# A one-core gated encoder block: the activation sums of h for the last stage move from the two-tile pool `t6` to the large pool

## The chip, the cores and the metric

The kernel runs on one core of a Trainium2 chip. The metric is device time in microseconds (us) of one execution. Before the change the median of three runs is 1447.47 us (1447.43 to 1447.57).

The engines have short names here. PE is TensorE (matmul) and PEld its loading of the stationary operand; DVE is VectorE; ACT is ScalarE; POOL is GpSimd; SP is SyncE, which issues most of the transfers. "PSUM" is the memory that matmuls write, "SBUF" the one that all other tiles lie in.

## The reference, cut to what matters

The block has 256 tokens of 2048 channels. Everything ahead of the feed-forward part (a gated recurrence, chunked attention, two projections and a merge) is untouched by the change and is left out:

```python
x = x + jnp.einsum('btd,de->bte', merged, w_out[l])
h = rms_norm(x, norm_ffn[l])
gate_up = jnp.einsum('btd,df->btf', h, w_ffn_in[l])      # 2048 -> 2 x 5632
ff_gate, ff_up = jnp.split(gate_up, 2, axis=-1)
x = x + jnp.einsum('btf,fd->btd', jax.nn.silu(ff_gate) * ff_up, w_ffn_out[l])
```

All arrays are float32.

## The kernel before

**The work.** Nearly all of it is matrix products of 256 tokens with weights that stream in once from device memory. A weight matrix is cut into blocks of 512 columns and chunks of 512 rows (four k-tiles of 128). A chunk of a block arrives in two transfers of 512 KB, issued by SP into `raw` tiles (pool `wraw`, eight tiles, line 124). To keep float32 precision with a fast matmul type, every operand is split into a high and a low part: ACT writes the high part (`whi`, lines 141 and 171) and DVE the low part, the difference (`wlo`, lines 142 and 172). The pools `whi` and `wlo` have four tiles each. A product of a k-tile is then three matmuls: high by high, high by low, low by high (lines 162 to 164, or 216 to 218 in `triple`).

**The feed-forward stage.** `hidden` has 11 blocks of 512 columns, `j` = 0 to 10. For each `j` the gate block and the up block are multiplied with x2 (the normalized input of the stage, tiles `x2Th`, `x2Tl`), and `hn` = silu(gate) * up results. For `j` in `SEVEN_IN` = (1, 3, 5, 7, 9) the two blocks are computed together by `product_pair`; for the others one after the other by `product` (lines 162 to 164). Then `transpose_split` transposes `hn` on PE (line 279) and splits it into `hTh` and `hTl`, which the last stage reads. It is a generator: each call of `tick` inside a product runs it one step further, so its steps lie beside the matmuls of the next `j`.

**Seven products for eight.** In `product_pair` the first two k-tiles of a chunk, the two halves of the tokens and the two column blocks form a 2x2 by 2x2 block product, done with seven products where eight are usual. For that, sums of weights and sums of activations are needed. `weight_forms` makes the sums of weights on DVE (line 188) from two `raw` tiles:

```python
        ta = t6_p.tile([P, 2, 512], F32, tag="t6", name=nm("ta"))
        tb = t6_p.tile([P, 2, 512], F32, tag="t6", name=nm("tb"))
        op(ta[:, 0, :], b12, b11, ALU.subtract)
        op(ta[:, 1, :], b22, b12, ALU.subtract)
        p5, p7 = halves(ta)
        op(tb[:, 0, :], ta[:, 0, :], b22, ALU.subtract)
        op(tb[:, 1, :], b21, tb[:, 0, :], ALU.add)
        p6, p4 = halves(tb)
```

`halves` splits each sum into `whi` (ACT) and `wlo` (DVE). Every pair of `SEVEN_IN` has four chunks, so four `ta` and four `tb`, and these take the two tiles of the pool `t6` in turn.

**The activation sums.** The last stage (`w_fo`) uses seven products for the chunks `j` in `SEVEN` = (1, 2, 3, 5, 6, 7, 9). The sums of h that it needs are made by `act_forms` when `hn` is transposed: one copy on ACT (line 325), four small sums on DVE (line 319) into a tile `sf`, then the split of `sf` into the tile `sform`, high part by ACT (line 171), low part by DVE (line 172). POOL's queue then writes `sform` to a buffer `kept` in device memory (line 309), and the last stage reads it back (line 846). A tile `sform` lives from its split to the landing of that write.

**The pools.** `big` has 33 tiles of 4 KB a partition, all with the tag `t4`; it holds x2, h, the sums `fx` of x2 and most else. `t6` has two tiles; before the change `sform` takes one of these two (line 836), the same that `ta` and `tb` take.

**What sets the order.** The program is written for a scheduler that orders each engine's instructions by priority and by when a tile of their pool is free; each engine then works through its own list in order and waits at semaphores. So the pool of a tile changes both what waits for what and where instructions stand. Of the seven `sform`, those of `j` = 2 and `j` = 6 come right ahead of a pair (`j` = 3 and `j` = 7), so that they are made while that pair's weight sums are made. `j` = 0, 4 and 8 make none, so the pairs 1, 5 and 9 begin without one.

Of the kernel before, what the change touches and what calls it, by code (L numbers as in the profile page):

```python
# [11 lines left out]
F32R = mybir.dt.float32r  # L12
# [5 lines left out]
P = 128  # L18
# [24 lines left out]
def block_kernel(ctx: ExitStack, tc: tile.TileContext, x, x_t, w_in, w_pa, w_pb, w_out, w_fi, w_fo,  # L43
# [8 lines left out]
    t6_p = ctx.enter_context(tc.tile_pool(name="t6", bufs=2))  # L52
# [7 lines left out]
    def nm(s):  # L60
        uid[0] += 1
        return f"{s}_{uid[0]}"

    def t4(shape, s, dt=F32):
        return big.tile(shape, dt, tag="t4", name=nm(s))
# [46 lines left out]
    def start(g):  # L112
        running.append(g)
# [33 lines left out]
    def product(w, nb, n_chunks, act, prologue=None, last=False):  # L147

        ps = [mm.tile([P, 512], F32, tag="mm", name=nm("mm")) for _ in range(2)]
        for kc in range(n_chunks):  # L150
            if prologue is not None:
                ws = load_weights(w, nb, kc, 1 if kc < 2 else 2, prologue(kc))
            else:
                with tc.high_priority(offset=min(PREP_AHEAD, tc.cur_priority - first_block[0])):
                    ws = load_weights(w, nb, kc)
            order = [(k4, m) for k4 in range(4) for m in range(2)]
            if last and kc == n_chunks - 1:
                order = [(k4, m) for m in range(2) for k4 in range(4)]
            for n, (k4, m) in enumerate(order):
                wh, wl = ws[k4]  # L160
                ah, al = act(kc * 4 + k4, m)
                nc.tensor.matmul(ps[m], lhsT=ah, rhs=wh, start=kc == 0 and k4 == 0, stop=False)  # L162
                nc.tensor.matmul(ps[m], lhsT=ah, rhs=wl, start=False, stop=False)  # L163
                nc.tensor.matmul(ps[m], lhsT=al, rhs=wh, start=False,  # L164
                                 stop=kc == n_chunks - 1 and k4 == 3)
                if n % 4 == 3:
                    tick()
        return ps
# [101 lines left out]
    def split_tiles(s):  # L270
        return (t4([P, 4, T], s + "h", F32R), t4([P, 4, T], s + "l", F32R))
# [29 lines left out]
    def transpose_split(nat, hi, lo, gain=None, wait=2, pool=aux, forms=None, spill=None):  # L301
        for _ in range(wait):
            yield 1
        for pair in range(2):
            pt = transpose_split_pair(nat, pair, hi, lo, gain, pool)
            if forms is not None and pair == 0:
                act_forms(pt, forms, gain)
                if spill is not None:
                    nc.gpsimd.dma_start(out=spill, in_=forms.bitcast(F32))
            yield 1  # L310
# [485 lines left out]
    def up_times(hn, m, up):  # L796
        nc.vector.scalar_tensor_tensor(out=hn[:, m, :], in0=up, scalar=r2[:, m:m + 1],
                                       in1=hn[:, m, :], op0=ALU.mult, op1=ALU.mult)

    def swiglu_pair(j):  # L800
        hn = t4([P, 2, 512], "hn")
        u = []

        def sums(ub):
            u.extend(t2([P, 512], "u") for _ in range(2))
            nc.scalar.copy(hn[:, 0, :], ub[1])
            add(u[0], ub[6], hn[:, 0, :])
            add(hn[:, 1, :], ub[7], u[0])
            add(u[1], ub[5], hn[:, 1, :])
            add(u[0], ub[5], u[0])  # L810

        cb = product_pair(w_fi, (j, NJ + j), 4, act_x2, fx, aux, mm, sums, plain_first=True,
                          last=True)
        for m in range(2):
            add(hn[:, m, :], cb[m, 0], hn[:, m, :])
            nc.scalar.activation(hn[:, m, :], hn[:, m, :], AF.Silu, scale=r2[:, m:m + 1])
        for m in range(2):
            add(u[m], cb[m, 1], u[m])
            up_times(hn, m, u[m])
        return hn  # L820

    for j in range(NJ):
        if j in SEVEN_IN:
            hn = swiglu_pair(j)
        else:
            ps = product(w_fi, j, 4, act_x2)
            hn = t4([P, 2, 512], "hn")
            for m in range(2):
                nc.scalar.activation(hn[:, m, :], ps[m], AF.Silu, scale=r2[:, m:m + 1])
            ps = product(w_fi, NJ + j, 4, act_x2)  # L830
            for m in range(2):
                up_times(hn, m, ps[m])
        hT.append(split_tiles("hT"))
        f = spill = None
        if j in SEVEN:
            f = t6_p.tile([P, 2, 4, P], F32R, tag="t6", name=nm("sform"))
            spill = kept[j] = dram.tile([P, 2, 4, P], F32, tag=f"kept{j}", name=nm("kept"))
        soon = dict(wait=0, pool=mm) if j + 1 in SEVEN_IN else {}
        start(transpose_split(hn, *hT[j], forms=f, spill=spill, **soon))
# [101 lines left out]
```

## Time and profile before

| | |
|---|---|
| median of 3 runs | 1447.47 us (1447.43 to 1447.57) |
| the profiled execution, its own time | 1449.29 us |
| span of its instructions | 1447.5 us |
| mean granted TensorE clock (1 is 2.4 GHz) | 0.995 |
| PE busy | 1431.1 us, 99% of the span |
| DVE, ACT, POOL busy | 990.4, 749.2, 48.5 us |
| transfers | 287.32 MB, mean 198 GB/s |

The span runs from the first instruction to the last; the execution's own time is 1.79 us longer, for what lies around it. Busy times of different engines overlap. Matmuls are pipelined: a matmul of 512 columns is recorded with 0.39 us, while the next one starts about 0.23 us after it, so an idle time between two records is about 0.16 us less than the distance of their starts lost.

### The profile page before, as it was taken

To read this page: it belongs to the slowest core of one execution; us is meant where nothing else is said; L and a number is where in the kernel's file an instruction comes from. 1 tells how busy PE (TensorE), PEld (TensorE's weight loads), DVE (VectorE), ACT (ScalarE), POOL (GpSimd) and SP (SyncE) were. 2 spreads that over 40 slices of the span, in tenths; PEclk is the share of its full clock that TensorE was granted. 3 is DMA by queue.
4 is the path that set the end of the run, shared out by engine and by line. 5 is a ranking of instruction groups with operands and counts; after the bars stand their busy time and mean duration, and the time that the engine had idled before them with its cause. 6 is when DMAs were issued, how large, how long until landed. Compare 5 with 4: busy or idle time off the path is not lost.

```text
span 1447.5 us, 17485 instructions
## 1 busy us (share of the span) xinstructions
PE 1431.1 (99%) x6484; PEld 1185.8 (82%) x6484; DVE 990.4 (68%) x1225; ACT 749.2 (52%) x966; POOL 48.5 (3%) x59
## 2 busy tenths in 40 slices
PE   8999999999999999999999999999999999999998
PEld 7888888888888888888888877888778888888887
DVE  6768869564654555556658768687686876777876
ACT  6756655555544444445555535455354554454553
POOL 0100100100000000100000000000000001000000
PEclk9999999999999999999999999999999999999999
DMA  9654454456556665556655646656466578666662
GB/s 356 235 196 154 137 198 148 168 172 207 181 198 203 203 192 191 189 183 218 204 194 177 227 150 213 208 178 228 147 216 207 178 236 314 230 200 224 203 190 85
DMA packets 81526, 287.32 MB, mean 198 GB/s; under 512 B 9120, under 2 KB 9376, under 8 KB 81440
## 3 DMA queue, kind: packets, MB, share of 16 engines
q1 hardware_dynamic: 78272, 274.66, 57.1%
q0 software_dynamic: 3168, 11.54, 2.1%
q8 instruction: 51, 0.84, 0.2%
q14 instruction: 35, 0.29, 0.1%
HBM read 278.30 MB, written 7.86 MB: 198 GB/s over the span
## 4 chain that ended last, share of the span: by engine, by line
PE 88%; issue 9%; DMA 1%; DVE 1%; ACT 0%; SPq 0%; POOL 0%; DVEq 0%; ACTq 0%; POOLq 0%
PE mm L162 19%; PE mm L164 19%; PE mm L163 19%; PE mp L216 9%; PE mp L217 9%; PE mp L218 9%; PE bank L279 2%; PE bank L537 1%; DMA xt<-in_x_t 1%; DMA kept<-sform 0%; PE bank L567 0%; PE bank L613 0%; PE bank L664 0%; ACT whi L171 0%; DVE tb L188 0%
## 5 line engine op out<-in xcount | busy, mean ns | idle before, releaser
L142 DVE TENSOR_TENSOR wlo<-raw,whi 128x1024 fp32r<-128x1024 f32 (+1 forms) x340 | 411.5, 1215 | 283.8 <-ACT whi L141 283.4
L141 ACT CAST whi<-raw 128x1024 fp32r<-128x1024 f32 (+1 forms) x340 | 352.9, 1042 | 384.6 <-PE mm L164 332.1
L162 PE MATMUL mm<-whi,xTh 128*128 128x512 f32 x704 | 276.9, 397 | 2.5 <-ACT whi L141 2.5
L164 PE MATMUL mm<-whi,xTl 128*128 128x512 f32 x704 | 274.9, 390 | 0.0
L163 PE MATMUL mm<-wlo,xTh 128*128 128x512 f32 x704 | 274.8, 390 | 0.0
L172 DVE TENSOR_TENSOR wlo<-raw,whi 128x1024 fp32r<-128x1024 f32 (+1 forms) x168 | 183.2, 1112 | 37.9 <-ACT whi L171 37.2
L171 ACT CAST whi<-raw 128x1024 fp32r<-128x1024 f32 (+1 forms) x168 | 157.0, 965 | 98.8 <-PE mp L218 53.6
L162 PEld LDWEIGHTS mm<-whi,xTh 128*128 128x128 f32 x704 | 132.1, 188 | 29.4 <-ACT whi L141 3.6
L164 PEld LDWEIGHTS mm<-whi,xTl 128*128 128x128 f32 x704 | 132.2, 188 | 27.6
L163 PEld LDWEIGHTS mm<-wlo,xTh 128*128 128x128 f32 x704 | 132.3, 188 | 26.9 <-DVE wlo L142 0.9
L162 PE MATMUL mm<-whi,x2Th 128*128 128x512 f32 x384 | 150.0, 391 | 0.0
L164 PE MATMUL mm<-whi,x2Tl 128*128 128x512 f32 x384 | 149.5, 389 | 0.0
L163 PE MATMUL mm<-wlo,x2Th 128*128 128x512 f32 x384 | 149.4, 389 | 0.0
L217 PE MATMUL mp<-wlo,hTh 128*128 128x512 f32 x282 | 109.7, 389 | 0.0
L218 PE MATMUL mp<-whi,hTl 128*128 128x512 f32 x282 | 109.6, 389 | 0.0
L216 PE MATMUL mp<-whi,hTh 128*128 128x512 f32 x282 | 99.7, 390 | 0.0
L218 PE MATMUL mp<-whi,x2Tl 128*128 128x512 f32 x220 | 87.5, 398 | 0.0
L217 PE MATMUL mp<-wlo,x2Th 128*128 128x512 f32 x220 | 87.4, 397 | 0.0
L164 PEld LDWEIGHTS mm<-whi,x2Tl 128*128 128x128 f32 x384 | 72.1, 188 | 15.0
L163 PEld LDWEIGHTS mm<-wlo,x2Th 128*128 128x128 f32 x384 | 72.1, 188 | 14.8
L162 PEld LDWEIGHTS mm<-whi,x2Th 128*128 128x128 f32 x384 | 72.1, 188 | 14.8
L216 PE MATMUL mp<-whi,x2Th 128*128 128x512 f32 x220 | 79.7, 405 | 0.0
(221 smaller groups left out, 1898.5 us busy)
## 6 DMA issues: line engine op xcount, KB each, us to landing
raw<-in_w_fi SPq DMA_DIRECT2D x176, 512.0 KB, 4.6
raw<-in_w_in SPq DMA_DIRECT2D x172, 512.0 KB, 4.4
raw<-in_w_fo SPq DMA_DIRECT2D x88, 512.0 KB, 5.0
raw<-in_w_out SPq DMA_DIRECT2D x32, 512.0 KB, 3.6
raw<-in_w_pa SPq DMA_DIRECT2D x16, 512.0 KB, 4.5
raw<-in_w_pb SPq DMA_DIRECT2D x16, 512.0 KB, 4.6
x<-x POOLq DMA_DIRECT2D x8, 512.0 KB, 4.6
kept<-sform POOLq DMA_DIRECT2D x7, 512.0 KB, 4.6
```

Source lines behind the costliest of these rows:

```text
L141: nc.scalar.copy(hi[:, sl, :], src[:, sl, :])
L142: nc.vector.tensor_tensor(out=lo[:, sl, :], in0=src[:, sl, :], in1=hi[:, sl, :].bitcast(F32), op=ALU.subtract)
L162: nc.tensor.matmul(ps[m], lhsT=ah, rhs=wh, start=kc == 0 and k4 == 0, stop=False)
L163: nc.tensor.matmul(ps[m], lhsT=ah, rhs=wl, start=False, stop=False)
L164: nc.tensor.matmul(ps[m], lhsT=al, rhs=wh, start=False, stop=kc == n_chunks - 1 and k4 == 3)
L171: nc.scalar.copy(hi, src)
L172: nc.vector.tensor_tensor(out=lo, in0=src, in1=hi.bitcast(F32), op=ALU.subtract)
L216: nc.tensor.matmul(ps, lhsT=ah, rhs=wh, start=first, stop=False)
L217: nc.tensor.matmul(ps, lhsT=ah, rhs=wl, start=False, stop=False)
L218: nc.tensor.matmul(ps, lhsT=al, rhs=wh, start=False, stop=final)
L279: nc.tensor.transpose(out=pt[:, j, m * P:(m + 1) * P], in_=nat[:, m, c:c + P], identity=ident)
L537: nc.tensor.matmul(pl[:, j, :], lhsT=ek[:, g // 2, (g % 2) * P:(g % 2 + 1) * P], rhs=eq[:, g, :], start=True, stop=True)
```

## The change

The tile `sform` is taken from the large pool, with the same shape and type. Nothing is computed otherwise, and no instruction is added or removed.

```diff
         hT.append(split_tiles("hT"))
         f = spill = None
         if j in SEVEN:
-            f = t6_p.tile([P, 2, 4, P], F32R, tag="t6", name=nm("sform"))
+            f = t4([P, 2, 4, P], "sform", F32R)
             spill = kept[j] = dram.tile([P, 2, 4, P], F32, tag=f"kept{j}", name=nm("kept"))
```

The order of instructions changes at the beginning of the pairs `j` = 3 and `j` = 7, in the same way, and nowhere else; SP's and POOL's lists stay as they are.

On DVE, at the beginning of the pair `j` = 3. `hTl_6764` is the low part of h of `j` = 2, `sf_6827` and `sform_6765` its activation sums; `ta_6890`, `tb_6891` are the weight sums of the pair's second chunk, made from `raw_6882` and `raw_6886`, and `wlo_6903`, `wlo_6909` their low parts. Before:

```order
L289 TENSOR_TENSOR hTl_6764<-bank_6850,hTh_6763 128x512
L319 TENSOR_TENSOR sf_6827<-bank_6820,sf_6827 128x128
L172 TENSOR_TENSOR wlo_6893<-raw_6882,whi_6892 128x1024
L319 TENSOR_TENSOR sf_6827<-bank_6820,sf_6827 128x128
L172 TENSOR_TENSOR wlo_6897<-raw_6886,whi_6896 128x512
L319 TENSOR_TENSOR sf_6827<-bank_6820,sf_6827 128x128 x2
L188 TENSOR_TENSOR ta_6890<-raw_6886,raw_6882 128x512
L188 TENSOR_TENSOR ta_6890<-raw_6886 128x512
L172 TENSOR_TENSOR sform_6765<-sf_6827,sform_6765 128x512
L172 TENSOR_TENSOR wlo_6903<-ta_6890,whi_6902 128x1024
L188 TENSOR_TENSOR tb_6891<-ta_6890,raw_6886 128x512
L188 TENSOR_TENSOR tb_6891<-raw_6882,tb_6891 128x512
```

With the change, on DVE at the same place, from the same h tile's second half on:

```order
L289 TENSOR_TENSOR hTl_6764<-bank_6850,hTh_6763 128x512
L319 TENSOR_TENSOR sf_6827<-bank_6820,sf_6827 128x128
L188 TENSOR_TENSOR tb_6891<-ta_6890,raw_6886 128x512
L172 TENSOR_TENSOR wlo_6893<-raw_6882,whi_6892 128x1024
L319 TENSOR_TENSOR sf_6827<-bank_6820,sf_6827 128x128
L172 TENSOR_TENSOR wlo_6897<-raw_6886,whi_6896 128x512
L319 TENSOR_TENSOR sf_6827<-bank_6820,sf_6827 128x128
L188 TENSOR_TENSOR tb_6891<-raw_6882,tb_6891 128x512
L172 TENSOR_TENSOR wlo_6903<-ta_6890,whi_6902 128x1024
L319 TENSOR_TENSOR sf_6827<-bank_6820,sf_6827 128x128
L172 TENSOR_TENSOR wlo_6909<-tb_6891,whi_6908 128x1024
```

The two `ta_6890` now stand ahead of the first row shown, before the first half of `hTl_6764`; both halves of `tb_6891` stand ahead of `wlo_6903` instead of behind it and behind `sform`; the low part of `sform_6765` comes four rows after the last row shown. On ACT the high part of `sform_6765` moves from ahead of `whi_6902` (from `ta`) to behind `whi_6908` (from `tb`) and the one cast that follows it.

On PE, at the same place (`mp` are the pair's PSUM banks, `fx` the sums of x2; `whi_6802` is from the first chunk's `tb`, `whi_6902` from `ta_6890`, `whi_6908` from `tb_6891`):

```order
 L218 MATMUL mp_6806<-whi_6892,x2Tl_5365 128x512
+L216 MATMUL mp_6867<-whi_6902,fx_5366 128x512
+L216 MATMUL mp_6871<-whi_6902,fx_5366 128x512
 L217 MATMUL mp_6836<-wlo_6897,fx_5366 128x512
 L218 MATMUL mp_6836<-whi_6896,fx_5366 128x512
-L216 MATMUL mp_6875<-whi_6802,fx_5183 128x512
-L217 MATMUL mp_6875<-wlo_6803,fx_5183 128x512
-L218 MATMUL mp_6875<-whi_6802,fx_5183 128x512
-L216 MATMUL mp_6867<-whi_6902,fx_5366 128x512
-L216 MATMUL mp_6871<-whi_6902,fx_5366 128x512
+L216 MATMUL mp_6810<-whi_6908,x2Th_5364 128x512
```

The first matmul that reads `whi_6908` now takes the place in PE's list that the last of the three matmuls with `whi_6802` and `wlo_6803` had: as many matmuls lie ahead of it as lay ahead of that one.

## Rows read from the trace of the kernel before

**Rows 1.** The page, busy time of each engine, share of the span, instructions.

```profile
PE 1431.1 (99%) x6484; PEld 1185.8 (82%) x6484; DVE 990.4 (68%) x1225; ACT 749.2 (52%) x966; POOL 48.5 (3%) x59
```

**Rows 2.** Waits of the whole span: engine, tile, releaser: total us, times, longest us.

```profile
PE mp L216 <- ACT whi L171: 7.8, 4, 3.0
...
DVE tb L188 <- DMA kept<-sform: 3.1, 2, 1.6
```

**Rows 3.** Windows, pairs j=1,3,5,7: length, busy PE PEld DVE ACT POOL, clock, DMA share, GB/s.

```profile
764.95:819.06 54.11, 54.11 (x243) 44.55 (x242) 46.15 (x55) 30.66 (x34) 0.00 (x0) 1.00 0.61 198
851.25:913.35 62.10, 57.75 (x243) 46.33 (x242) 48.06 (x60) 31.21 (x36) 0.53 (x1) 0.95 0.55 181
945.52:999.62 54.10, 54.10 (x243) 44.55 (x242) 46.16 (x55) 30.62 (x34) 0.00 (x0) 1.00 0.60 200
1031.79:1094.10 62.31, 57.85 (x244) 46.45 (x243) 48.07 (x60) 31.23 (x36) 0.53 (x1) 0.95 0.53 180
```

**Rows 4.** Timeline of PE, pair j = 3: start us, duration us, [idle before, releaser].

```profile
864.20 0.39 PE L218 MATMUL mp<-whi,fx 128*128 128x512 f32 x1
865.54 0.73 PE L216 MATMUL mp<-whi,fx 128*128 128x512 f32 x2 [0.96 <-ACT whi L171]
866.80 0.50 PE L217 MATMUL mp<-wlo,fx 128*128 128x512 f32 x1 [0.53 <-DVE wlo L172]
...
867.61 0.40 PE L218 MATMUL mp<-whi,fx 128*128 128x512 f32 x1
870.87 0.79 PE L216 MATMUL mp<-whi,fx 128*128 128x512 f32 x1 [2.86 <-ACT whi L171]
```

**Rows 5.** Timeline of DVE and ACT, pair j = 3, at the same place.

```profile
860.42 0.28 DVE L319 TENSOR_TENSOR sf<-bank,sf 128x128 f32<-128x128 f32 x1
860.62 1.21 DVE L172 TENSOR_TENSOR wlo<-raw,whi 128x1024 fp32r<-128x1024 f32 x1
...
864.28 0.68 DVE L172 TENSOR_TENSOR sform<-sf,sform 128x512 fp32r<-128x512 f32 x1
...
865.52 1.23 DVE L172 TENSOR_TENSOR wlo<-ta,whi 128x1024 fp32r<-128x1024 f32 x1 [0.56 <-ACT whi L171]
...
868.24 0.69 DVE L188 TENSOR_TENSOR tb<-ta,raw 128x512 f32<-128x512 f32 x1 [1.49 <-DMA kept<-sform]
868.97 0.69 DVE L188 TENSOR_TENSOR tb<-raw,tb 128x512 f32<-128x512 f32 x1
...
869.77 1.04 ACT L171 CAST whi<-tb 128x1024 fp32r<-128x1024 f32 x1 [4.28 <-DVE tb L188]
```

**Rows 6.** Windows in pair j = 3, columns as in rows 3.

```profile
872.00:876.00 4.00, 4.00 (x11) 3.19 (x11) 4.00 (x6) 2.28 (x3) 0.00 (x0) 0.50 0.76 269
877.00:878.00 1.00, 1.00 (x6) 0.80 (x5) 0.28 (x1) 0.00 (x0) 0.00 (x0) 1.00 0.85 283
```

**Rows 7.** Timeline of DVE and ACT, pair j = 5, the corresponding instructions.

```profile
950.78 0.69 DVE L188 TENSOR_TENSOR ta<-raw,raw 128x512 f32<-128x512 f32 x1
...
954.70 0.68 DVE L188 TENSOR_TENSOR tb<-ta,raw 128x512 f32<-128x512 f32 x1
...
957.03 0.68 DVE L188 TENSOR_TENSOR tb<-raw,tb 128x512 f32<-128x512 f32 x1
957.83 1.05 ACT L171 CAST whi<-tb 128x1024 fp32r<-128x1024 f32 x1 [1.23 <-DVE tb L188]
```

**Rows 8.** POOL's last write and first reads of the sums, and their first use on PE.

```profile
1186.17 0.53 POOL L309 DMA_DIRECT2D kept<-sform  x1 [85.73 <-DVE sform L172]
1186.86 2.37 POOL L846 DMA_DIRECT2D sf<-kept  x4 [0.16 <-issue]
...
1225.73 0.39 PE L216 MATMUL mp<-whi,sf 128*128 128x512 f32 x1
```

**Rows 9.** The page, DMA issues: count, KB each, median us to landing.

```profile
kept<-sform POOLq DMA_DIRECT2D x7, 512.0 KB, 4.6
sf<-kept POOLq DMA_DIRECT2D x7, 512.0 KB, 10.7
```

**Rows 10.** An early wait of PE, and the clock around it (timeline; window).

```profile
7.57 0.73 PE L162 MATMUL mm<-whi,xTh 128*128 128x512 f32 x2 [1.76 <-ACT whi L141]
...
6.00:8.00 2.00, 0.43 (x2) 0.30 (x2) 0.96 (x4) 1.07 (x2) 0.00 (x0) 1.00 0.99 306
```

## The prediction, made before the changed kernel was run

> **What bounds the kernel now.** I read first the busy times: PE works 1431.1 of 1447.5 us [rows 1], so only what PE loses by waiting, or by a slower clock, can be won back without taking work away. Next I read the waits of the whole span and look for those whose waiting engine is PE or whose releaser is the tile that the change moves. There are two such lines [rows 2]: PE waits 7.8 us, in four waits, for a high part of weights that ACT writes in `product_pair`; and DVE's sums `tb` wait, twice, 1.6 us at most, for the write of `sform` to device memory.
>
> Third, the windows of the pairs show whether these belong together and what they cost. A pair is the same work each time, so the pairs whose predecessor makes no `sform` are controls for those with one. The controls `j` = 1 and 5 last 54.11 and 54.10 us with a granted clock of 1.00; `j` = 3 and 7 last 62.10 and 62.31 us at 0.95 [rows 3]. The excess over 54.10 is 8.00 and 8.21 us, **16.21 us** in all.
>
> Fourth, the timelines of the pair `j` = 3 take the 8.00 apart. A matmul of the control takes 54.10 / 243 = 0.22 us. PE starts at 864.20, 865.54, 866.80 (two matmuls after the one before), 867.61 and 870.87 [rows 4]: 1.34 - 0.22 = 1.12, then 1.26 - 0.44 = 0.82, then 3.26 - 0.22 = 3.04 us lost, 4.98 together. The missing 8.00 - 4.98 = 3.02 us are the clock: after the long wait PE works at a granted clock of 0.50, that is 1.2 GHz, and by 877 it is back at 1.00, 2.4 GHz [rows 6].
>
> Why PE waits stands on DVE and ACT [rows 5]. DVE makes the low part of `sform` at 864.28, POOL writes it out, and only when that has landed may `tb` of the second chunk take its tile, at 868.24. Its second half follows at 868.97, ACT's cast `whi<-tb` at 869.77, and PE's matmul at 870.87. In the control the second half of `tb` runs at 957.03 and the cast at 957.83 [rows 7]. Moved by 851.25 - 945.52 = -94.27 us, the distance of the two pairs' starts, these are 862.76 and 863.56: six microseconds earlier. The first two losses have the same root: `ta` stands late in DVE's list, because its tile was expected late; in the control it starts at 950.78 [rows 7], 856.51 in the time of `j` = 3.
>
> **The change, part by part.** Instructions and transfers stay the same in number and kind; `sform` takes a tile of `big`, and `ta`, `tb` have `t6` to themselves. All costs are sums against the profiled execution, span 1447.5 us, 1449.29 us with what lies around it; since the excess is a difference inside one span, I take it off the median, 1447.47 us.
>
> *What goes:* the wait of `tb` for the landing, the late `ta`, and the slow clock behind them: 16.21 us, if the pairs 3 and 7 came out as the controls.
>
> *What stays:* they can't come out quite so, since four sums `sf` and the split of `sform` still lie on DVE here, and not in the controls. In the new order three of the sums stand ahead of the second half of `tb`. One takes 0.20 us from start to start (860.42 to 860.62 [rows 5]), so `tb` is 0.60 later than in the control: 863.36, the cast 863.56 + 0.60 = 864.16, its end 1.05 later, 865.21. PE started 0.06 after such a cast (870.87 against 869.77 + 1.04 [rows 4, 5]), so 865.27. In PE's new order the matmul that reads this tile has the place of the one that started at 864.20 [rows 4]. PE loses 1.07 us there, or in parts at one of the waits just ahead. Two sites: **2.14 us**.
>
> Bounds of this term: it is zero if the DVE work is hidden, as in the control; at the most it is the first two losses of before, 1.12 + 0.82 = 1.94 us per site, the nearest rows for a wait on these sums without the transfer. I take 1.07, from the order.
>
> *The rest of the sums.* The fourth `sf` and the low part of `sform` (0.68 [rows 5]) make DVE 0.80 + 0.68 = 1.48 us later than in the control. PE itself is then 1.07 late, so 0.41 is left, and DVE is busy 46.16 of the control's 54.10 us [rows 3], so this is hidden. If that cover is gone it costs 0.41 per site. ACT's cast of `sform` moves behind `whi<-tb`; ACT is busy 30.62 of 54.10 us.
>
> *The spill* is issued some 5 us later, behind the later split. Nobody waits for it now but the last stage, hundreds of microseconds on: nothing.
>
> *POOL's reloads.* The tiles of `big` are handed out in another turn. The fourth of the seven reloads waits, in the new program, for the landing of the last spill: 1186.17 + 4.6 = 1190.8 us, where it was issued by about 1189 [rows 8, 9]. With 10.7 us to land [rows 9] it is there at 1201.5, and PE's first use of any reloaded sum is at 1225.73 [rows 8]. So 24 us cover it: nothing.
>
> *Room in `big`.* At `j` = 9, the fullest, 8 tiles of x2, 20 of h, `hn` and `sform` are alive, 30 of 33; the four `fx` are used up. At `j` = 7 it is 8 + 4 + 16 + 2 = 30. No new wait for room.
>
> **Sum:** 16.21 - 2.14 = 14.07 us less: 1447.47 - 14.07 = **1433.4 us**, with own ends 1447.47 - 16.21 = 1431.3 and 1431.3 + 2 x (1.94 + 0.41) = 1436.0.
>
> **The rivals.**
>
> *The clock falls all the same.* PE would still have a wait at this place of each pair, and if that were enough to drop to 1.2 GHz, each site would keep its 3.02 us: 1436.4 us with one site, 1439.4 with both. For it: the fall of before came behind waits at just this place. Against it: the fall shows behind a loss of 3.04 us that followed 1.94, while at 7.57 us PE had waited 1.76 us and the window around it shows a clock of 1.00 [rows 10]; the wait to come, 1.07, is shorter. Chance 0.09.
>
> The Trainium skill, "TensorE: Matmul & The Clock Gate", section "A second HAM failure mode: psum-queue depth-cycling", speaks against this change's full gain: there, short idles of TensorE between groups of matmuls, while it cycled through PSUM banks, were enough to throw the clock back and forth. By that rule the time would be the 1439.4 of this rival; rows 10 disagree for a single wait of 1.76 us.
>
> *The change doesn't do what it says:* what held `tb` was not the spill but something that ends as late, so that the same wait stands under another name, and the time stays at 1447.5. For it: a wait for several semaphores is put down to the last one alone. Against it: the control makes the same `tb` six microseconds earlier with the same weights' transfers. Chance 0.02.
>
> *Slower: the reload in the last stage.* The spill's tile now belongs to the pool that the reloads draw on, and behind the fourth reload three more and those of x2 stand in POOL's queue. If the last spill landed so late that PE had to wait for a reloaded sum, the time could exceed the old one. Its place is PE's matmul at 1225.73, and it decides when the wait exceeds the 14.07 us saved: the fourth reload would have to land after 1225.73 + 14.07 = 1239.8, 38 us later than worked out above. Slower by that much and 3 more would be 1450.5 us. Spills take 4.6 us, reloads 10.7 [rows 9]; nothing speaks for it. Chance 0.02.
>
> **How the numbers follow.** The forecast has 0.87. A measurement of this kernel tells a change from none at about 0.2%, 2.9 us, that is below 1444.6 or above 1450.4. The forecast and the clock rival lie below, 0.96; the second rival within, 0.02; the third above, 0.02. The range runs from the forecast's lower end to its upper end and takes in the clock's fall at one site: 1431.2 to 1436.5.
>
> **What would show it.** In the profile after, the line of DVE's `tb` waiting for `kept<-sform` is gone; the windows of pairs 3 and 7, found again by their matmuls, last 55.2 us (54.1 to 56.4), with a clock of 1.00; PE's wait for `whi` there is about 1 us once per pair, where three waits stood. The last stage keeps its length. I am wrong if a pair still lasts over 57 us, if the clock falls inside one, if PE waits for a reloaded `sf`, or if another pair than 3 and 7 changes its length.

## The result, and the profile after

| | before | after |
|---|---|---|
| median, same session | 1447.52 us (1447.43 to 1447.62, 4 runs) | 1435.46 us (1435.22 to 1436.35, 4 runs) |
| the profiled execution, its own time | 1449.29 us | 1435.26 us |
| its span | 1447.5 us | 1433.5 us |

The ratio is 0.9918, 95% interval 0.9901 to 0.9935: **12.06 us faster**. Forecast were 14.07 us and 1433.4; the result lies 2.1 us above that, inside the range of 1431.2 to 1436.5. In one later session one execution of the changed kernel took 2219.24 us at a mean granted clock of 0.606; it is left out of what is said there.

The page after, busy time of each engine, answers to [rows 1], and the chain that ended last now runs through PE for 98% of the span, 88% before:

```profile
PE 1425.6 (99%) x6484; PEld 1183.0 (83%) x6484; DVE 989.9 (69%) x1225; ACT 749.1 (52%) x966; POOL 48.5 (3%) x59
...
PE 98%; DVE 1%; ACT 0%; DMA 0%; issue 0%; SPq 0%; DVEq 0%; ACTq 0%
```

The same instructions in number. PE's busy time fell by 1431.1 - 1425.6 = 5.5 us. A matmul is busy for longer at a clock of 0.50, 0.63 us at 872.41 in the trace of before where 0.39 is usual, and in the pairs 3 and 7 those have gone.

The waits of the kernel after: for PE all that the view lists, and of POOL's the one that is new (total us, times, longest us), against [rows 2]:

```profile
PE mm L162 <- ACT whi L141: 1.6, 1, 1.6
PE warm_ps L92 <- DVE warm L89: 1.2, 1, 1.2
PE mp L216 <- ACT whi L171: 1.1, 2, 0.5
...
POOL sf L846 <- DMA kept<-sform: 2.7, 1, 2.7
```

PE's 7.8 us in four waits have become 1.1 in two, none over about half a microsecond, and no `tb` waits for `kept` any more. The last line is the fourth reload of the last stage, which waits for the landing of the last spill, as foretold.

The windows of the five pairs (columns as in [rows 3]; the fifth is `j` = 9):

```profile
764.93:819.02 54.09, 54.09 (x243) 44.55 (x242) 46.16 (x55) 30.62 (x34) 0.00 (x0) 1.00 0.58 197
851.21:906.42 55.21, 54.67 (x243) 44.40 (x242) 47.45 (x60) 31.28 (x36) 0.53 (x1) 1.00 0.61 202
938.59:992.68 54.09, 54.09 (x244) 44.55 (x243) 46.16 (x55) 30.61 (x34) 0.00 (x0) 1.00 0.59 196
1024.85:1080.04 55.19, 54.67 (x243) 44.40 (x242) 47.45 (x60) 31.27 (x36) 0.53 (x1) 1.00 0.63 204
1112.21:1166.33 54.12, 54.12 (x243) 44.55 (x242) 46.16 (x55) 30.62 (x34) 0.00 (x0) 1.00 0.59 197
```

Pairs 3 and 7 went from 62.10 and 62.31 us to 55.21 and 55.19, with a clock of 1.00 throughout; against 54.10 an excess of 1.11 and 1.09 us is left. The other pairs keep their length.

At the kernel's beginning, though, the clock does fall in this profile, where PE has waited 1.64 us (timeline; window):

```profile
7.19 0.73 PE L162 MATMUL mm<-whi,xTh 128*128 128x512 f32 x2 [1.64 <-ACT whi L141]
...
9.00:12.00 3.00, 3.00 (x9) 2.33 (x8) 1.93 (x4) 2.21 (x5) 0.00 (x0) 0.50 1.03 397
```

The kernel before waited 1.76 us there [rows 10] and its clock stayed at 1.00. It costs nothing in the end: the 43rd matmul behind the wait starts at 18.75 us, before at 18.77.

DVE, ACT and PE in pair 3, the kernel after, in order of time; they answer to [rows 4, 5]:

```profile
860.38 0.28 DVE L319 TENSOR_TENSOR sf<-bank,sf 128x128 f32<-128x128 f32 x1
860.58 0.68 DVE L188 TENSOR_TENSOR tb<-ta,raw 128x512 f32<-128x512 f32 x1
...
862.31 0.28 DVE L319 TENSOR_TENSOR sf<-bank,sf 128x128 f32<-128x128 f32 x1
...
863.11 0.28 DVE L319 TENSOR_TENSOR sf<-bank,sf 128x128 f32<-128x128 f32 x1
...
863.31 0.68 DVE L188 TENSOR_TENSOR tb<-raw,tb 128x512 f32<-128x512 f32 x1
...
864.10 1.05 ACT L171 CAST whi<-tb 128x1024 fp32r<-128x1024 f32 x1 [0.68 <-DVE tb L188]
864.27 0.39 PE L218 MATMUL mp<-whi,fx 128*128 128x512 f32 x1
...
865.20 0.50 PE L216 MATMUL mp<-whi,x2Th 128*128 128x512 f32 x1 [0.54 <-ACT whi L171]
...
868.72 0.68 DVE L172 TENSOR_TENSOR sform<-sf,sform 128x512 fp32r<-128x512 f32 x1
```

The first half of `tb` starts at 860.58 instead of 868.24, with nothing to wait for. Three `sf` sums of 0.20 us each stand ahead of the second half, and that makes the cast late and PE with it: 865.20 - 864.27 = 0.93 us from start to start where a matmul takes 0.22, so 0.71 us are lost at this place; the rest of the 1.1 is smaller losses just beside it. The low part of `sform`, and with it the spill, now comes at 868.72, and nobody is waiting for it.

### The profile page after: what moved, and what is told of

The parts are those of the page before. It is cut to its first block, busy times and chain, and to the rows that moved or that the text cites. A ratio compares the mean times of both kernels' runs of the same rounds, so it can differ in the third digit from the quotient of the medians.

```text
span 1433.5 us, 17475 instructions
## 1 busy us (share of the span) xinstructions
PE 1425.6 (99%) x6484; PEld 1183.0 (83%) x6484; DVE 989.9 (69%) x1225; ACT 749.1 (52%) x966; POOL 48.5 (3%) x59
## 4 chain that ended last, share of the span: by engine, by line
PE 98%; DVE 1%; ACT 0%; DMA 0%; issue 0%; SPq 0%; DVEq 0%; ACTq 0%
PE mm L164 21%; PE mm L162 21%; PE mm L163 21%; PE mp L217 10%; PE mp L216 10%; PE mp L218 10%; PE bank L279 2%; PE bank L537 1%; DVE wlo L172 0%; PE bank L567 0%; DMA raw<-in_w_in 0%; ACT whi L171 0%; PE bank L613 0%; PE bank L664 0%; PE bank L692 0%; DVE tb L188 0%
```

## The experiments

Nine kernels ran. The diffs of e1, e2, e4, e5 and e8 are against the kernel before; e6 and e10 are built on the change, and e9 on e6. Two lengths of a pair are used: the window of [rows 3], 54.10 us in a control, and the one from the pair's first matmul to the first matmul of the next plain product, 39.57 us in a control.

My theory was that of the prediction: the landing of the spill holds `tb`; the shared pool also puts `ta` late in DVE's order; both keep PE waiting and the longest of these waits brings the clock down; after the change only the `sf` sums are left. The rivals were that the clock or the landing plays no part of its own, and that it matters which pool the tile comes from.

### e1: the kernel before, once more

No edit: how much does the excess of a pair vary from one execution to the next?

> The kernel before, profiled once more, to see whether its profiled execution (1449.29 us) stands for its ordinary ones (1447.5). Theory: what varies between executions is the slow clock at the pairs 3 and 7. In an ordinary execution the stretches at a clock of 0.50 are shorter, the mean clock is above the 0.995 of the first profile, and the two pairs together exceed 2 x 54.10 us by some 14.4 us (16.21 less the 1.8 that the first profile was longer). Rival: the excess of the pairs is 16.2 us in every execution, and the 1.8 us lie elsewhere, at the kernel's start or end.

Measured: 1447.53 us (1445.88 to 1448.85, 10 runs). Its profiled execution took 1447.62 us. Its pairs 3 and 7, windows:

```profile
851.14:912.16 61.02, 56.62 (x243) 45.38 (x242) 48.08 (x60) 31.22 (x36) 0.53 (x1) 0.97 0.56 183
...
1030.61:1092.39 61.78, 57.31 (x244) 46.03 (x242) 48.07 (x60) 31.22 (x36) 0.53 (x1) 0.94 0.55 181
```

PE's waits are those of [rows 2] to a tenth (7.8, 4, 3.0), but the excess is 6.92 + 7.68 = 14.60 us where the first profile had 16.21. What differs is how long PE worked at the lower clock. Two stretches of pair 3 in this run:

```profile
872.00:874.00 2.00, 2.00 (x5) 1.62 (x6) 2.00 (x3) 1.57 (x2) 0.00 (x0) 0.50 0.73 256
874.00:876.00 2.00, 2.00 (x9) 1.63 (x8) 2.00 (x3) 0.62 (x1) 0.00 (x0) 0.85 0.76 250
```

In the first profile the clock was 0.50 until 876 [rows 6]; here its mean is 0.85 from 874 to 876, so that for most of this stretch it is back at 1.00. So at pair 3 the waits are a fixed cost, 4.98 us in both, and the clock behind them is one that varies: 6.92 - 4.98 = 1.94 us here, 3.02 in the first profile.

### e2: the change for `j` = 2 alone

```diff
-            f = t6_p.tile([P, 2, 4, P], F32R, tag="t6", name=nm("sform"))
+            f = (t4([P, 2, 4, P], "sform", F32R) if j == 2 else
+                 t6_p.tile([P, 2, 4, P], F32R, tag="t6", name=nm("sform")))
```

> Only j = 2 takes its sums from the large pool, j = 6 and the others stay in the two-tile pool. Theory: the sites are independent, so pair 3 lasts about 55.1 us and pair 7 stays at 61 to 62.3, and half of the 12.06 us measured for the whole change goes: 1441.5 us (1440.5 to 1442.5). Rival: the change works through something shared (room in the pool, the order of the last stage): all or nothing, 1435.5 or 1447.5 us.

Measured: 1441.53 us (1440.86 to 1442.77), ratio to before 0.9954 [0.9939, 0.9968], and the windows of pairs 3 and 7:

```profile
850.43:905.61 55.18, 54.66 (x243) 44.40 (x242) 47.47 (x60) 31.27 (x36) 0.53 (x1) 1.00 0.62 202
...
1024.02:1085.86 61.84, 57.38 (x243) 46.07 (x242) 48.07 (x60) 31.25 (x36) 0.53 (x1) 0.94 0.53 181
```

Pair 3 is that of the change, pair 7 that of before: the two sites are independent, and each is worth about half of the gain. Pairs 1, 5 and 9 last 54.07 to 54.09 us, as ever.

### e8: the pool of before, the spill from another tile

```diff
                 if spill is not None:
-                    nc.gpsimd.dma_start(out=spill, in_=forms.bitcast(F32))
+                    nc.gpsimd.dma_start(out=spill.rearrange("p a b c -> p (a b c)"),
+                                        in_=x2T[0][0].rearrange("p a t -> p (a t)").bitcast(F32))
```

> The sums stay in the two-tile pool, but the write to device memory reads a tile of x2 instead (so the last stage multiplies with wrong sums); the sums' tile is free as soon as it is made. Theory: the long wait (3.04 us per site, for the landing) goes, and with it the clock's fall; the late weight sums stay: 1.12 + 0.82 us and up to 1 us more per site, so that the pairs 3 and 7 last 56 to 57.2 us at a clock of 1.00 and the whole 1438 to 1441 us. Rival one, the place in DVE's order is all of it, the landing hides behind it: the pairs stay above 60 us and the time above 1444. Rival two, the landing is all of it: pairs at 55.1 us and 1435.5 us as with the change.

Measured: 1440.87 us (1440.03 to 1441.86), ratio 0.9948 [0.9933, 0.9963]. Pair 3's window, and the start of `ta` on DVE in it:

```profile
853.02:910.57 57.55, 55.21 (x243) 44.32 (x242) 47.89 (x60) 31.18 (x36) 0.00 (x0) 1.00 0.55 186
...
864.85 0.68 DVE L188 TENSOR_TENSOR ta<-raw,raw 128x512 f32<-128x512 f32 x1
```

The same row in the kernel before:

```profile
863.08 0.68 DVE L188 TENSOR_TENSOR ta<-raw,raw 128x512 f32<-128x512 f32 x1
```

PE's matmuls in e8's pair 3 with the three longest of its waits, from the timeline:

```profile
867.32 0.73 PE L216 MATMUL mp<-whi,fx 128*128 128x512 f32 x2 [0.96 <-ACT whi L171]
...
868.66 0.50 PE L217 MATMUL mp<-wlo,fx 128*128 128x512 f32 x1 [0.60 <-DVE wlo L172]
...
870.41 0.50 PE L216 MATMUL mp<-whi,fx 128*128 128x512 f32 x1 [0.56 <-ACT whi L171]
```

Here `ta` stands as late as before: 864.85 - 853.02 = 11.83 us behind the pair's start, before 863.08 - 851.25 = 11.83. The first two waits are 0.96 and 0.60 us, in [rows 4] 0.96 and 0.53; the third is down from 2.86 to 0.56, and the clock stays at 1.00. The excess is 57.55 - 54.10 = 3.45 us in pair 3 and 3.46 in pair 7, a little over what I expected. This splits a site of e1 (7.30 us on average): the landing and the clock that falls behind its wait take 7.30 - 3.45 = 3.85; the late place of `ta` and `tb` on DVE 3.45 - 1.10 = 2.35; and 1.10 are what the change leaves. The split is not quite clean. The first half of `tb` now stands ahead of `wlo<-ta` on DVE, behind it before, and as nothing holds the writes any more they all go out at 669 to 672 us, so that no transfer of sums lies in the pair; the change and e5 have that transfer in the pair and come out at 55.2 us all the same, so its mere presence is not what costs. The pool of a tile costs through the order, too, not through the wait alone.

### e4: each spill issued twice

```diff
                     nc.gpsimd.dma_start(out=spill, in_=forms.bitcast(F32))
+                    nc.gpsimd.dma_start(out=spill, in_=forms.bitcast(F32))
```

> The kernel before with each write of sums to device memory issued twice, so that the tile in the two-tile pool is held until the second has landed. Theory: the landing is on PE's path at the pairs 3 and 7; the second write waits for the first and takes as long (2.9 us from issue to landing), so each of the two pairs grows by 2.5 to 4 us, more where the clock stays low for longer, and the whole by 5 to 9 us: 1453 to 1457 us. Rival: the landing is hidden behind the late weight sums, which alone hold PE: the time stays within 1 us of the kernel before.

Measured: 1453.47 us (1453.08 to 1456.5), ratio 1.004 [1.0027, 1.0053]. The second write goes out when the first has landed, so the tile is held about twice as long. DVE and PE in pair 3, from the timeline:

```profile
871.41 0.69 DVE L188 TENSOR_TENSOR tb<-ta,raw 128x512 f32<-128x512 f32 x1 [5.04 <-DMA kept<-sform]
...
874.04 0.80 PE L216 MATMUL mp<-whi,fx 128*128 128x512 f32 x1 [6.42 <-ACT whi L171]
```

And the pair's window:

```profile
850.87:915.35 64.48, 56.57 (x244) 45.52 (x242) 48.07 (x60) 31.22 (x36) 1.07 (x2) 0.95 0.54 183
```

DVE waits 5.04 - 1.49 = 3.55 us longer than in [rows 5], PE 6.42 - 2.86 = 3.56 longer than in [rows 4], and the pair is 64.48 - 61.02 = 3.46 longer than in e1 (pair 7: 65.07 - 61.78 = 3.29). Microsecond for microsecond the landing is on PE's path. By the medians the two sites together give 5.55 us (1453.47 against 1447.92), less than 2 x 3.55 = 7.1; the varying clock lies in both medians, and whether it is the whole of the difference is not shown.

### e5: a tile of its own, not one of the large pool

```diff
-    big = ctx.enter_context(tc.tile_pool(name="big", bufs=33))
+    big = ctx.enter_context(tc.tile_pool(name="big", bufs=32))
...
+    sform_p = ctx.enter_context(tc.tile_pool(name="sform", bufs=1)); ...
...
-            f = t6_p.tile([P, 2, 4, P], F32R, tag="t6", name=nm("sform"))
+            f = sform_p.tile([P, 2, 4, P], F32R, tag="sform", name=nm("sform"))
```

> The sums of h take neither pool: a pool of their own with one tile, and the large pool gives up one of its 33. Theory: all that counts is that the sums' tile is not one of the two that the weight sums need; the pairs 3 and 7 last 40.65 us as with the change, at a clock of 1.00, and the ratio to before is 0.990 to 0.993. Rival: the change's gain depends on the large pool's many tiles, since the sums of two j follow each other at a distance; then pairs with sums wait for the one tile, or another stage waits for the large pool's 32, and the time is 1437 us or more.

Measured: 1435.27 us (1434.83 to 1435.64), ratio 0.9913 [0.9897, 0.993]; the windows of pairs 3 and 7:

```profile
851.15:906.35 55.20, 54.66 (x243) 44.40 (x242) 47.47 (x60) 31.26 (x36) 0.53 (x1) 1.00 0.62 203
...
1024.79:1080.02 55.23, 54.68 (x244) 44.40 (x242) 47.48 (x60) 31.27 (x36) 0.53 (x1) 1.00 0.62 203
```

This is the change's result. The large pool brings nothing of its own; what counts is that `sform` no longer shares `t6`. The reload's wait for the last spill, which only the large pool can bring, also makes no difference.

### e6 and e9: the sums on POOL

What is left, 1.1 us a site, I put down to the `sf` sums ahead of `tb`. e6 takes them off DVE: ACT copies the transposes out of PSUM, POOL makes the four sums and the low part of `sform`, for all seven `j`.

```diff
-                nc.vector.tensor_tensor(out=out, in0=x, in1=y, op=o)
+                nc.gpsimd.tensor_tensor(out=out, in0=x, in1=y, op=o)
...
+            c = t4([P, 2, T], "pc")
+            nc.scalar.copy(c, pt)
...
+            nc.scalar.copy(f[:, 0], s)
+            nc.gpsimd.tensor_tensor(out=f[:, 1], in0=s, in1=f[:, 0].bitcast(F32),
+                                    op=ALU.subtract)
```

> The change, and in addition the activation sums of h are made by POOL from a copy in a tile of the large pool that ACT writes, so that four small sums and the low part of their split leave DVE, for all seven j. Theory: the wait that is left in the pairs 3 and 7 comes from the three sums ahead of the weight sum on DVE; without them the pairs last 54.1 to 54.4 us, 1.6 to 1.9 us in all less than with the change: 1433.6 us (1433.2 to 1434.5). Rival: POOL's work slows DVE's instructions while both run, or the bank of the transposes comes free later: 1435.5 us or more.

Measured: 1436.3 us (1435.53 to 1436.93), ratio 0.9916 [0.9901, 0.9931]; pair 3 lasts 55.69 us, an excess of 1.59 where the change has 1.11. The expectation failed, though DVE now has five instructions less in the pair (x55). DVE and POOL, in order of time:

```profile
863.62 0.68 DVE L188 TENSOR_TENSOR tb<-raw,tb 128x512 f32<-128x512 f32 x1
863.88 1.58 POOL L338 TENSOR_TENSOR sform<-sf,sform 128x512 fp32r<-128x512 f32 x1 [0.73 <-ACT sform L337]
864.22 2.32 DVE L172 TENSOR_TENSOR wlo<-ta,whi 128x1024 fp32r<-128x1024 f32 x1
866.46 1.21 DVE L172 TENSOR_TENSOR wlo<-tb,whi 128x1024 fp32r<-128x1024 f32 x1
```

DVE's subtraction takes 2.32 us where the next one, of the same shape, takes 1.21. It starts while POOL's subtraction runs, and POOL ends at 863.88 + 1.58 = 865.46, that is 866.54 - 865.46 = 1.08 us ahead of DVE's end: as though it had begun only then. The Trainium skill, "SBUF — State Buffer", section "🔬 SBUF: two separate sides", states that these two engines share a port pair which the one that starts first holds for its whole instruction, and that a DVE operation with two SBUF inputs is blocked by a GpSimd operation that reads SBUF; this pair of rows agrees with it.

e9 tells whether that one instruction of POOL is to blame: it is e6 with the low part of `sform` back on DVE.

```diff
-            nc.scalar.copy(f[:, 0], s)
-            nc.gpsimd.tensor_tensor(out=f[:, 1], in0=s, in1=f[:, 0].bitcast(F32),
-                                    op=ALU.subtract)
+            split(f[:, 0], f[:, 1], s)
```

> As the kernel with all sums on POOL, but the low part of the split stays on DVE, so that POOL has only the four small sums. Theory: in that kernel one DVE subtraction took 2.32 us where others take 1.22, while POOL's subtraction of 128x512 ran (863.88 to 865.46): both engines have two inputs in SBUF and one waits for the other. Without POOL's long instruction the pairs 3 and 7 come out at 40.1 to 40.4 us, against 41.17 with it, and the whole 1.5 to 2 us less than that kernel, 0.6 to 1.2 us less than the change. Rival: the long subtraction was held by something else, and the pairs stay at 41 us or more.

Measured: 1435.1 us (1434.21 to 1435.57), ratio 0.9909 [0.9894, 0.9924]; the pair lasts 55.18 us, or 40.67 to the next plain product, where 40.1 to 40.4 were expected. DVE at the same place:

```profile
860.68 0.78 DVE L188 TENSOR_TENSOR tb<-ta,raw 128x512 f32<-128x512 f32 x1
861.38 2.35 DVE L172 TENSOR_TENSOR wlo<-raw,whi 128x1024 fp32r<-128x1024 f32 x2
863.65 0.68 DVE L188 TENSOR_TENSOR tb<-raw,tb 128x512 f32<-128x512 f32 x1
864.25 1.21 DVE L172 TENSOR_TENSOR wlo<-ta,whi 128x1024 fp32r<-128x1024 f32 x1
865.39 0.68 DVE L172 TENSOR_TENSOR sform<-sf,sform 128x512 fp32r<-128x512 f32 x1
865.99 1.21 DVE L172 TENSOR_TENSOR wlo<-tb,whi 128x1024 fp32r<-128x1024 f32 x1
```

The 2.32 us are 1.21 again, so POOL's long subtraction was the cause in e6. Still the pair gains nothing over the change: the second half of `tb` starts no earlier than with the sums on DVE (863.65 - 851.50 = 12.15 us into the pair, with the change 863.31 - 851.21 = 12.10), and the low part of `sform` now stands ahead of `wlo<-tb`. In the control the two halves of `tb` start 957.03 - 954.70 = 2.33 us apart [rows 7]; here it is 863.65 - 860.68 = 2.97, though no sum lies between them, because two `wlo` of 128x1024 stand there, 2.35 us against the 1.82 of the control's two. Work taken off an engine was replaced by other work at the same place in its list.

### e10 and e11: the sums later, beside the change itself

e10 leaves the sums on DVE and changes when: for `j` = 2 and 6 ACT copies the transposes to a tile of `big`, and the sums are made 14 ticks later. e11 is the change once more, beside it.

```diff
             if forms is not None and pair == 0:
...
+                if wait == 0:
+                    late = t4([P, 2, T], "late")
+                    nc.scalar.copy(late, pt)
...
+        if forms is not None and wait == 0:
+            for _ in range(14):
+                yield 1
+            act_forms(late, forms, gain)
+            nc.gpsimd.dma_start(out=spill, in_=forms.bitcast(F32))
```

> The change, and for j = 2 and 6 ACT copies the transposes to a tile of the large pool and the sums are made from it on DVE in the third and fourth chunk of the pair. Theory: what is left in the pairs 3 and 7 (1.1 us each) is DVE's work on the sums ahead of the second chunk's weight sums; moved behind them the pairs last as those without sums, 39.6 us, and the whole 2.0 to 2.3 us less than the change in this group. Rival: the chunk in which the sums are now made waits instead, pairs at 40.3 us or more and less than 1 us gained.

> The change once more, beside the other kernels of this group and more executions of the kernel before. Theory: the pairs 3 and 7 last 40.7 us from the first matmul of the pair to the next plain product, 1.1 us above the pairs without sums, with no slow clock in them, in every execution; what the ordinary executions of before and after differ by is then the excess of before less 2.2 us, where that excess varies from execution to execution between some 13 and 16 us: a ratio of 0.990 to 0.993.

Measured: e11 1434.56 to 1436.62 us, ratio 0.9908 [0.989, 0.9926], both pairs 55.16 us. e10 1432.77 us (1431.93 to 1433.5), ratio 0.9893 [0.9878, 0.9908]. e10's waits of PE over the whole span:

```profile
PE mm L162 <- ACT whi L141: 1.7, 2, 1.2
PE warm_ps L92 <- DVE warm L89: 1.2, 1, 1.2
```

Its pairs 3 and 5 up to the next plain product, windows:

```profile
850.14:889.70 39.56, 39.56 (x179) 32.59 (x178) 34.34 (x40) 23.34 (x27) 0.00 (x0) 1.00 0.52 179
936.38:975.95 39.57, 39.57 (x179) 32.59 (x178) 34.34 (x40) 22.95 (x26) 0.00 (x0) 1.00 0.53 180
```

Pair 3 is as long as its control, with the same 40 instructions on DVE, and no wait of `product_pair` is left: the sums now run behind the pair, where DVE starts them at 893.66:

```profile
893.66 0.28 DVE L328 TENSOR_TENSOR sf<-late,sf 128x128 f32<-128x128 f32 x1
```

(A window as in [rows 3] holds 247 matmuls of PE in e10's order instead of 243, so the shorter length is compared.) So making and splitting the sums at this place was the whole of the 1.1 us that the change leaves at each site. That it costs through DVE is read from the order of the rows and not shown by e10 alone, which moves ACT's cast of `sform` and the spill along. The mean of e11's four executions is 1435.34 us, 2.6 above e10, of which the pairs give 2 x 1.1 = 2.2; the rest is less than the spread of either. e10 is faster than both kernels.

## Why the prediction was right, point by point

- **What holds `tb`: right.** The line of `tb` waiting for `kept<-sform` is gone, e4 lengthens it and the pair with it, and e8 takes it away alone. The rival that something else ends as late has fallen.
- **"What stays", 1.07 us a site: right**, 1.11 and 1.09 measured. The second half of `tb`, the cast and PE's matmul were put at 863.36, 864.16 and 865.27; they came at 863.31, 864.10 and 865.20, in a pair that begins 0.04 earlier. That it is the work on the sums is shown by e10; that it is DVE's part of it, by the rows alone.
- **"Nothing" for the spill, the reloads and room in `big`: right.** The fourth reload waits 2.67 us for the last spill's landing, and PE's first use of a reloaded sum moved from 1225.73 [rows 8] to 1211.71, by 14.02 us, as the whole did. e5 shows the same without the large pool.
- **The clock rival: fell, but not by the argument against it.** It needed a fall behind waits of about 1 us a pair; the clock was 1.00 there in the change, and also in e8 with 3.45 us lost in several waits of 0.96 at most. Inside the pairs it fell only where one wait was 2.86 us or more. The Trainium skill, "TensorE: Matmul & The Clock Gate", section "A second HAM failure mode: psum-queue depth-cycling", by which short idles between groups of matmuls were enough in another kernel, is not borne out in these pairs. The prediction's argument was that a wait of 1.76 us had left the clock at 1.00 [rows 10]. That window ends at 8.00 us; the changed kernel also shows 1.00 from 6 to 8, and then 0.50 from 9 to 12, after a wait of only 1.64. So a wait of this length can go either way, and that the argument came out right is luck in part.
- **The slower rival: fell.** No wait of PE for a reloaded `sf` is in the list.
- **The sum: 2 us too much, and the step that failed is** "since the excess is a difference inside one span, I take it off the median". Against the profiled execution the working holds: 1449.29 - 14.07 = 1435.22, measured 1435.26. But the profiled execution of before was 1449.29 - 1447.47 = 1.82 us longer than the median, and the extra time lay in the very thing that the change removes, the stretches at 1.2 GHz. The term "what goes" was therefore mis-sized for the median: 16.21 us in that execution, 14.60 in e1's, whose own time is 1449.29 - 1447.62 = 1.67 us shorter, which is this difference of 1.61 almost alone; and by the medians 12.06 + 2.20 = 14.26. Taken off the profiled execution's own time, as the clock's share of the term asks for, the same working gives 1435.2. That the range took the error in is luck too: its upper end was made for the sums' wait and for the clock's fall at one site, and nothing in it was meant for the variation between executions.

## What to carry to other kernels

A tile that waits for a transfer out should not share a small pool with tiles that feed the bounding engine: the landing then lies on that engine's path, and the scheduler, expecting the tile late, puts other work late as well; in this kernel a tile of the large pool (the change) or one of its own (e5) did instead. Where a gain includes time at a lower clock, take it off the time of the execution in which it was measured, or profile twice: waits repeat to a tenth of a microsecond, stretches at a low clock don't. And work on an engine that isn't the bound still costs where it stands ahead of what the bound waits for; moving it in time (e10) took that away, moving it to another engine (e6, e9) did not. All this is shown for one kernel.

## What the runs showed of the hardware that I had not expected

- In two profiled executions of the same program, with the same waits, PE worked for different stretches at 1.2 GHz (a granted clock of 0.50): 6.92 and 8.00 us of excess at pair 3, 7.68 and 8.21 at pair 7. The executions of before spread over 1445.66 to 1450.53 us, at a mean granted clock of 0.997 for the shortest and 0.993 for the longest; those of the change over 1434.56 to 1436.62.
- A DVE subtraction of 128x1024 took 2.32 us instead of 1.21 beside a POOL subtraction that was running when it began (e6); beside POOL's four smaller sums only single operations grew, `tb` from 0.68 to 0.78 us. POOL's own instructions grew as well: in the two pairs of e6 its third and fourth sum took 2.31 us together and its subtraction 1.58 and 1.57, for the other five `j` 1.85 to 1.89 and 1.29 to 1.30.
- At the kernel's beginning the granted clock of the profile and the lengths of the matmuls can disagree: in e8 matmuls of 512 columns take 0.63 us each from 9.31 to 13.15 us, the length seen elsewhere at 0.50, while the profile shows 1.00.
